# Making the first FFN weight sums earlier, in a pool of their own, and taking the FFN's other sums off GpSimd

## The chip, the cores and the metric

The kernel runs on one core of a Trainium2 chip. The metric is the device time of one execution in microseconds; the median of the runs shown counts. The engines are called by their names or by the abbreviations of the profile: TensorE (PE), VectorE (DVE), ScalarE (ACT), GpSimd (POOL) and SyncE (SP), which issues the weight loads.

## The reference

One trunk layer on x of 512 frames by 1024 features, in float32. The change lies in the feed-forward network (FFN) at its end, where D_FF is 2816:

```python
def reference(x, ...):
    ...
        h = h + (g_a * ya + g_b * yb) @ w_o[l]
        hn = rmsnorm(h, norm_ffn_g[l])
        gu = hn @ w_ffn_in[l]
        g, up = jnp.split(gu, 2, axis=-1)
        h = h + (jax.nn.silu(g) * up) @ w_ffn_out[l]
    return rmsnorm(h, final_norm_g)
```

Ahead of it stand a norm, one wide input projection, chunked band attention, an RG-LRU branch and the gated merge of the two.

## The kernel before, in words

**Products in three parts.** Every float32 operand is split into a high part (`hi`, rounded by a ScalarE copy) and a low part (`lo`, the rest, by a VectorE subtraction; `split`, lines 78 to 81). A product is three matmuls, hi·hi, hi·lo and lo·hi (`mm3`, lines 72 to 76). So each weight tile costs one load on SP's queue, one ScalarE copy and one VectorE subtraction before TensorE may use it, and the lo·hi matmul needs the subtraction as well.

**Weights.** `chunks` lists all weight blocks in order of use. `load` issues 512 KB into a `raw` buffer of the pool `wp` (three buffers; every fourth load of the FFN's Strassen blocks goes to a single buffer of the pool `sc`). `prefetch` keeps the split weights (`whl`, four buffers in `wp`) ahead of their use.

**The stage of w_o** (lines 746 to 763): four row tiles by two column halves; each psum result is added to `h` on VectorE (line 756), squared and summed on ScalarE. After two row tiles the FFN norm's first half follows (`norm_half`, TensorE transposes at line 326), and the second half later.

**The FFN's first two blocks** fg0 and fu0 are multiplied plainly, half of the rows before and half after the second norm half (`po_f0` to `po_f3`).

**The FFN's other blocks**, fg2, fu2, fg4 and so on to fu20, use a Strassen–Winograd scheme: seven products in place of eight. It needs four sums of the activations, t1 to t4 (lines 810 to 820: `sum_t`, split into `bt0` to `bt3`), and for each block four sums of its weight quarters (`weight_sums`, lines 158 to 188): s1 = a21 + a22, s2 = s1 − a11, s3 = a11 − a21, s4 = a12 − s2. The plain quarters a11, a12 and a22 and the four sums are each split. `block_product` (lines 240 to 263) then runs seven products of 12 matmuls (128x128 by 128x256). One psum tile, `p`, gathers a11·b11, + s2·t2, + s3·t3, + a22·t4, and after each of them ScalarE copies the state so far (`keepa`, `keepb`, c); the other, `q`, takes a12·b21, s1·t1 and s4·b22:

```python
        product(p[:], w["s2"], right["t2"], False)
        keep(a[:, 1], p[:])
        product(q[:, 1], w["s1"], right["t1"], True)
        keep(b[:, 0], q[:, 1])
        product(p[:], w["s3"], right["t3"], False)
        keep(b[:, 1], p[:])
```

**What sets the order.** A planner orders the instructions of each engine before the kernel runs, so the order in the profile can differ from the program's; each engine then works through its list in order. Buffers come free tile by tile: whoever needs one waits until the last reader of its former tile is done.

**What GpSimd does in the FFN before:** s3 and s4 of fg2, fu2 and fg4 (lines 172 and 173), the four operations of t3 and t4 (line 805, called from 813 and 814), and the low part of `bt3` (line 819).

Of the kernel before, what the change touches and what calls it, by code (L numbers as in the profile page):

```python
# [8 lines left out]
F32 = mybir.dt.float32  # L9
F32R = mybir.dt.float32r  # L10
# [4 lines left out]
P = 128  # L15
# [17 lines left out]
CW = 256  # L33
# [3 lines left out]
def block_kernel(ctx: ExitStack, tc: tile.TileContext, x, norm_mix_g, w_in, b_merge, rel_table,  # L37
# [3 lines left out]
    pe, dve, act, pool, sp = nc.tensor, nc.vector, nc.scalar, nc.gpsimd, nc.sync  # L41

    def pool_of(name, bufs=1, side="left"):
        return tc.tile_pool(name=name, bufs=bufs, side=side, reuse_waits="tile")

    def opened(name, bufs=1, side="left"):
        st = ExitStack()
        return st, st.enter_context(pool_of(name, bufs, side))
# [6 lines left out]
    wp = ctx.enter_context(pool_of("wp", 2))  # L55
# [10 lines left out]
    def f(ap):  # L66
        return ap.bitcast(F32)

    def mm_tile(name, tag="mm"):
        return ps.tile([P, S], F32, tag=tag, bufs=4 if tag == "mm" else 2, name=name)  # L70
# [7 lines left out]
    def split(hi, lo, src):  # L78

        act.activation(hi, src, AF.Copy)  # L80
        dve.tensor_sub(lo, src, f(hi))  # L81
# [52 lines left out]
    raws = {}  # L134
    extra = {}

    def load(name, k):
        _, parts, rows, kts = chunks[index[name]]
        wide = sum(width for *_, width in parts)
        n = min(4 * CW // wide, kts - k)  # L140
        at = rows + k * P
        pl, bufs = wp, 3
        if name in strassen and name[0] == "f":
            loads[0] += 1
            pl, bufs = (room[0], 1) if loads[0] % 4 == 0 else (wp, 3)
        raw = pl.tile([P, n, wide], F32, tag="raw", bufs=bufs, name=f"raw_{name}_{k}")
        to = 0
        for src, col, width in parts:
            sp.dma_start(out=raw[:, :, to:to + width],
                         in_=src[at:at + n * P, col:col + width].rearrange("(k p) e -> p k e", p=P))  # L150
            to += width
        raws[name, k] = raw

    slots, loads = [0], [0]
    barrier = ["wo1"]
    room = [None]

    def weight_sums(name):

        for k in (0, 4):  # L160
            if (name, k) not in raws:
                load(name, k)
        r0, r1 = raws.pop((name, 0)), raws.pop((name, 4))
        a11, a21, a12, a22 = r0[:, :, 0:P], r0[:, :, P:CW], r1[:, :, 0:P], r1[:, :, P:CW]
        sc = room[0]
        s21, s34 = (sc.tile([P, 2, 4, P], F32, tag=tag, bufs=1, name=f"{tag}_{name}")
                    for tag in ("s21", "s34"))
        s2, s1, s3, s4 = s21[:, 0], s21[:, 1], s34[:, 0], s34[:, 1]
        dve.tensor_add(s1, a21, a22)
        dve.tensor_sub(s2, s1, a11)  # L170
        other = pool if name in ("fg2", "fu2", "fg4") else dve
        other.tensor_sub(s3, a11, a21)
        other.tensor_sub(s4, a12, s2)
        blocks_ = {}
        for group in ((("a11", a11), ("a12", a12)), (("s2", s2), ("s1", s1)), (("s3", s3), ("s4", s4)), (("a22", a22),)):
            pl, tag, bufs = sc, "a22", 2
            if len(group) == 2:
                slots[0] += 1
                pl, tag, bufs = (sc, "whl", 1) if slots[0] % 5 == 0 else (wp, "whl", 4)
            o = pl.tile([P, len(group), 2, 4, P], F32R, tag=tag, bufs=bufs, name=f"whl_{name}_{group[0][0]}")  # L180
            together = group[0][0] in ("s2", "s3") and name != "fg2"
            if together:
                split(o[:, :, 0], o[:, :, 1], (s21 if group[0][0] == "s2" else s34)[:])
            for i, (key, src) in enumerate(group):
                if not together:
                    split(o[:, i, 0], o[:, i, 1], src)
                blocks_[key] = o[:, i]
        return blocks_

    def prefetch(n):  # L190
        while len(made) < min(n, len(chunks), index.get(barrier[0], len(chunks))):
            name, parts, rows, kts = chunks[len(made)]
            if name in strassen:
                made.append(weight_sums(name))
                continue
            tiles = []
            wide = sum(width for *_, width in parts)
            step = 4 * CW // wide
            for k in range(0, kts, step):
                n_ = min(step, kts - k)  # L200
                if name in extra:
                    hl = extra[name].tile([P, 2, n_, wide], F32R, tag="whl", bufs=4, name=f"whl_{name}_{k}")
                else:
                    hl = wp.tile([P, 2, n_, wide], F32R, tag="whl", bufs=4, name=f"whl_{name}_{k}")
                if (name, k) not in raws:
                    load(name, k)
                raw = raws.pop((name, k))
                if len(made) == 0 and k:
                    act.activation(hl[:, 0], raw[:], AF.Copy)
                    pool.tensor_sub(hl[:, 1], raw[:], f(hl[:, 0]))  # L210
                else:
                    split(hl[:, 0], hl[:, 1], raw[:])
                tiles.append(hl)
            made.append(lambda part, k, at, tiles=tiles, step=step: tiles[k // step][:, part, k % step, at])

    def weights(name, ahead=1):
        prefetch(index[name] + 1 + ahead)
        return made[index[name]]
# [116 lines left out]
    def features(pl, tag, name):  # L335

        t = pl.tile([P, KT, 2, S], F32R, tag=tag, name=name)
        return t, [t[:, k] for k in range(KT)]
# [13 lines left out]
    _, xnT = features(xnp, "xn", "xnT")  # L352
# [361 lines left out]
    _, mT = features(xnp, "xn", "mT")  # L714
# [16 lines left out]
        act.dma_start(out=ht[t][:], in_=x[t * P:(t + 1) * P, :])  # L731


    x32_stack, x32p = opened("x32", 1, "right")
    bl = {(kh, half): (x32p if (kh, half) == (0, 1) else hnp).tile([P, 2, 4, 256], F32R, name=f"hn{kh}{half}")
          for kh in range(2) for half in range(2)}
# [7 lines left out]

    hsq = []
    prefetch(index["wo1"] + 1)
    for t in range(NT):
        q2 = cp.tile([P, 2], F32, tag="hsq2", bufs=2, name=f"hsq2_{t}")
        for cc in range(2):
            wo = weights(f"wo{cc}", 0)  # L750
            po = mm_tile(f"po_h{cc}_{t}")
            for k in range(KT):
                mm3(po[:], mT[k][:, 0, t * P:(t + 1) * P], mT[k][:, 1, t * P:(t + 1) * P],
                    wo(0, k, every), wo(1, k, every), k == 0, k == KT - 1)
            hs = ht[t][:, cc * S:(cc + 1) * S]
            dve.scalar_tensor_tensor(hs, po[:], 0.5, hs, ALU.mult, ALU.add)
            junk = tg_.tile([P, S], F32, tag="tg", name=f"hj{t}_{cc}")
            act.activation(junk[:], hs, AF.Square, accum_out=q2[:, cc:cc + 1])
        q = cp.tile([P, 1], F32, tag="ssq", bufs=4, name=f"hsq{t}")
        dve.tensor_reduce(q[:], q2[:], mybir.AxisListType.X, ALU.add)  # L760
        hsq.append(q[:])
        if t == 1:
            norm_half(x32p, ht, hsq, gf, hn_at, 0, "ffn", f_at)
# [2 lines left out]


    acp = ctx.enter_context(pool_of("act", 13))
    bt_stack, btp = opened("bt")
    act2 = []  # L770

    def act_tile(j):
        o = acp.tile([P, 2, S], F32, tag="act", name=f"act{j}")
        act2.append(o)
        return o
# [20 lines left out]
    def sums(name):  # L796
        t = acp.tile([P, 4, 256], F32, tag="act", name=f"sum_{name}")
        return t

    def of_x(kh, half, i):  # L800
        return x32[2 * kh + i][:, :, half * 256:half * 256 + 256]

    def halves_of(dst, op, in0, in1):
        for i in range(2):
            op(dst[:, 2 * i:2 * i + 2], in0(i), in1(i))

    def own_half(t):
        return lambda i: t[:, 2 * i:2 * i + 2]

    t1, t2, t3, t4 = (sums(f"t{i}") for i in range(1, 5))  # L810
    halves_of(t1, dve.tensor_sub, lambda i: of_x(0, 1, i), lambda i: of_x(0, 0, i))
    halves_of(t2, dve.tensor_sub, lambda i: of_x(1, 1, i), own_half(t1))
    halves_of(t3, pool.tensor_sub, lambda i: of_x(1, 1, i), lambda i: of_x(0, 1, i))
    halves_of(t4, pool.tensor_sub, lambda i: of_x(1, 0, i), own_half(t2))
    bt = []
    for i, t in enumerate((t1, t2, t3, t4)):
        o = btp.tile([P, 2, 4, 256], F32R, name=f"bt{i}")
        act.activation(o[:, 0], t[:], AF.Copy)
        (pool if i == 3 else dve).tensor_sub(o[:, 1], t[:], f(o[:, 0]))
        bt.append(o)  # L820
    hn_right = right_side(lambda kh, half, part, k: bl[kh, half][:, part, k], bt)
    x32_stack.close()
    sc_stack, sc = opened("sc", 2)
# [23 lines left out]
    for j in range(2, FT, 2):  # L847
# [4 lines left out]
        o = act_tile(j)[:].rearrange("p a b -> p (a b)")  # L852
# [2 lines left out]
        dve.tensor_mul(o, o, u[:].rearrange("p a b -> p (a b)"))  # L855
    sc_stack.close()
    bt_stack.close()
    hn_stack.close()


# [97 lines left out]
```

## Time and profile before

| | |
|---|---|
| median of 3 runs | 892.38 us (891.75 to 892.43) |
| the profiled execution | 892.82 us |
| its span, first to last instruction | 891.0 us |
| mean granted TensorE clock | 0.996 |
| TensorE busy | 875.7 us (98%) |
| VectorE busy | 553.5 us (62%) |
| ScalarE busy | 473.2 us (53%) |
| GpSimd busy | 130.2 us (15%) |

The times and tables below come from one profiled execution. In a timeline a row has the start and the duration in us, the engine, the source line, the operation and its output and inputs by the program's names without numbers; in square brackets at the end stands how long the engine had idled before, and what ended that. Rows of several like instructions in sequence are merged (x2 and so on). Group rows have the count, then the busy time in us and the mean of one in ns. The stage of w_o runs from about 486 to 532 us, the FFN's plain blocks up to 556, the Strassen blocks from there to about 768, and the output projection from 760 on.

### The profile page before, as it was taken

The numbers are of one execution on the slowest core, as the hardware profiler recorded it, in microseconds if no ns is written. First come the engines' busy times: TensorE is split into PE (matmuls) and PEld (weight loads), VectorE is DVE, ScalarE is ACT, GpSimd is POOL, SyncE is SP. The second block draws the span as 40 slices with busy tenths as digits, with TensorE's granted clock in tenths as the row PEclk, the third lists the DMA queues.
The fourth block names the chain that finished last, engine by engine and source line by source line (L and its number), as shares of the span: only waits on it lengthen the run. The fifth ranks groups of instructions, "written<-read, shape, count | busy, mean of one in ns | idle before, by whom it ended". The sixth has DMA issues, their size and how long they took to land.

```text
span 891.0 us, 13319 instructions
## 1 busy us (share of the span) xinstructions
PE 875.7 (98%) x5220; PEld 779.4 (87%) x5220; DVE 553.5 (62%) x863; ACT 473.2 (53%) x841; POOL 130.2 (15%) x168
## 2 busy tenths in 40 slices
PE   8999999999999999999999999899999999999997
PEld 5988888888889889898888889899999999888886
DVE  5777557563466675666456356998788887463203
ACT  7566646652266676667434366556655556723203
POOL 4012112120022222323000003400000001300200
PEclk9999999999999999999999999899999999999999
DMA  8323223333332232331224430333333333253102
GB/s 264 89 79 111 82 91 95 120 95 95 106 104 74 77 101 72 94 96 61 71 85 145 172 95 25 95 119 116 122 95 95 97 115 101 97 187 125 37 1 96
DMA packets 85024, 89.06 MB, mean 100 GB/s; under 512 B 5344, under 2 KB 73552, under 8 KB 84960
## 3 DMA queue, kind: packets, MB, share of 16 engines
q1 hardware_dynamic: 83584, 84.73, 30.7%
q10 hardware_dynamic: 1376, 3.47, 1.0%
q8 instruction: 41, 0.67, 0.3%
q14 instruction: 23, 0.19, 0.1%
HBM read 86.05 MB, written 2.14 MB: 99 GB/s over the span
## 4 chain that ended last, share of the span: by engine, by line
PE 94%; DVE 3%; ACT 1%; issue 1%; DMA 1%; POOL 0%; SPq 0%; ACTq 0%
PE po_out L74 5%; PE po_out L76 5%; PE po_out L75 5%; PE p_fu L75 2%; PE p_fu L74 2%; PE o L663 2%; PE p_fu L76 2%; PE p_fg L75 2%; PE p_fg L76 2%; PE p_fg L74 2%; PE pT L643 2%; PE po_v L76 2%; PE po_v L75 2%; PE po_v L74 2%; PE po_q L74 2%; PE q_fg L76 2%
## 5 line engine op out<-in xcount | busy, mean ns | idle before, releaser
L75 PE MATMUL po_out<-whl_fo,act_hi 128*128 128x512 f32 (+1 forms) x198 | 72.4, 366 | 0.0
L74 PE MATMUL po_out<-whl_fo,act_hi 128*128 128x512 f32 (+1 forms) x198 | 72.4, 366 | 0.0
L76 PE MATMUL po_out<-whl_fo,act_lo 128*128 128x512 f32 (+1 forms) x198 | 71.6, 365 | 0.0
L631 POOL TENSOR_SCALAR p<-p,rl 128x128 f32<-128x128 f32 (+1 forms) x64 | 35.9, 583 | 142.0 <-DVE rl L629 142.0
L81 DVE TENSOR_TENSOR whl_fo<-raw_fo,whl_fo 128x1024 fp32r<-128x1024 f32 x22 | 27.6, 1261 | 45.5 <-ACT whl_fo L80 45.1
L80 ACT ACTIVATE whl_fo<-raw_fo 128x1024 fp32r<-128x1024 f32 x22 | 22.9, 1056 | 49.3 <-PE po_out L76 35.0
L627 DVE CUSTOM_DVE_ANT_0 p<-s,bias 128x384 f32<-128x384 f32 (+2 forms) x64 | 29.5, 484 | 21.5 <-PE s L625 20.9
L76 PEld LDWEIGHTS po_out<-whl_fo,act_lo 128*128 128x128 f32 x198 | 37.3, 189 | 6.0
L75 PEld LDWEIGHTS po_out<-whl_fo,act_hi 128*128 128x128 f32 x198 | 37.4, 189 | 6.0
L74 PEld LDWEIGHTS po_out<-whl_fo,act_hi 128*128 128x128 f32 x198 | 37.4, 189 | 6.0
L628 ACT ACTIVATE p<-p,m 128x384 f32<-128x384 f32 (+2 forms) x64 | 35.7, 560 | 12.6 <-DVE m L627 12.2
L843 POOL TENSOR_TENSOR act_lo<-act,act_hi 128x1024 fp32r<-128x1024 f32 x4 | 10.5, 2621 | 185.9 <-ACT act_hi L842 184.4
L76 PE MATMUL po_v<-whl_v,xnT 128*128 128x256 f32 x128 | 36.2, 283 | 0.0
L75 PE MATMUL po_v<-whl_v,xnT 128*128 128x256 f32 x128 | 36.1, 282 | 0.0
L74 PE MATMUL po_v<-whl_v,xnT 128*128 128x256 f32 x128 | 36.1, 282 | 0.0
L81 DVE TENSOR_TENSOR pp<-pT,pp 128x512 fp32r<-128x512 f32 (+1 forms) x64 | 29.3, 484 | 5.3 <-ACT pp L80 5.0
L81 DVE TENSOR_TENSOR whl_fu_s<-s_fu,whl_fu_s 128x1024 fp32r<-128x1024 f32 x20 | 25.3, 1280 | 5.8 <-ACT whl_fu_s L80 5.7
L75 PE MATMUL po_xr<-xnT,whl_xr 128*128 128x512 f32 (+1 forms) x80 | 27.9, 354 | 0.6 <-DVE xnT L331 0.6
L74 PE MATMUL po_gr<-xnT,whl_gr 128*128 128x512 f32 (+1 forms) x80 | 27.8, 349 | 0.1
L76 PE MATMUL po_gr<-xnT,whl_gr 128*128 128x512 f32 (+1 forms) x80 | 27.5, 348 | 0.3 <-DVE whl_gr L81 0.3
L75 PE MATMUL po_gr<-xnT,whl_gr 128*128 128x512 f32 (+1 forms) x80 | 27.6, 346 | 0.0
L74 PE MATMUL po_xr<-xnT,whl_xr 128*128 128x512 f32 (+1 forms) x80 | 26.6, 351 | 0.8 <-ACT xnT L330 0.8
(354 smaller groups left out, 3077.1 us busy)
## 6 DMA issues: line engine op xcount, KB each, us to landing
raw_fg<-in_w_ffn_in_dram SPq DMA_DIRECT2D x22, 512.0 KB, 4.4
raw_fu<-in_w_ffn_in_dram SPq DMA_DIRECT2D x22, 512.0 KB, 3.5
raw_fo<-in_w_ffn_out_dram SPq DMA_DIRECT2D x22, 512.0 KB, 4.0
raw_qk<-in_w_in_dram SPq DMA_DIRECT2D x32, 256.0 KB, 3.2
raw_xr<-in_w_in_dram SPq DMA_DIRECT2D x8, 512.0 KB, 4.6
raw_gr<-in_w_in_dram SPq DMA_DIRECT2D x8, 512.0 KB, 3.5
raw_ga<-in_w_in_dram SPq DMA_DIRECT2D x8, 512.0 KB, 3.9
raw_gb<-in_w_in_dram SPq DMA_DIRECT2D x8, 512.0 KB, 3.5
```

The costliest lines, as they stand in the source:

```text
L74: pe.matmul(o, sh, mh, start=start, stop=False, skip_group_check=parts)
L75: pe.matmul(o, sh, ml, start=False, stop=False, skip_group_check=parts)
L76: pe.matmul(o, sl, mh, start=False, stop=stop, skip_group_check=parts)
L80: act.activation(hi, src, AF.Copy)
L81: dve.tensor_sub(lo, src, f(hi))
L627: dve.tensor_tensor_reduce(prob[qb][:], sc[:, 0:w], bias[:, S - w:S], -1.0, 3e38, ALU.add, ALU.min, nmax[:, qb:qb + 1])
L628: act.activation(prob[qb][:], prob[qb][:], AF.Exp, bias=nmax[:, qb:qb + 1], scale=-1.0, accum_out=lsum[:, qb:qb + 1])
L631: pool.tensor_scalar(prob[qb][:], prob[qb][:], rl[:, qb:qb + 1], 1.0, ALU.mult, ALU.mult)
L643: pe.transpose(pt[:, at * P:(at + 1) * P], prob[qb][:, kb * P:(kb + 1) * P], ident[:])
L663: pe.matmul(po[:, S - n:S], st, pp[i][:, part, lo:lo + n], start=kb == 0 and part == 0, stop=kb == NT - 1 and part == 1)
L843: (pool if i in (0, 1, 2, 4) else dve).tensor_sub(lo[:], o[:], f(hi[:]))
```

## The change

A new pool `sums` is opened on the right side before the norm's tiles and closed after the Strassen blocks. It holds the two tiles of sums (`s21`, `s34`) of every block, and one buffer of split weights that the pool `sc` held before.

`weight_sums("fg2", True)` is called right behind the prefetch of w_o. It loads fg2 (two loads of 512 KB), makes its four sums, splits s2 and s1 in one piece and keeps s3 and s4. When fg2's turn comes in `prefetch`, its weights are loaded a second time, for a11, a12 and a22, which now go into spare tiles of the activation pool (`acp`); s3 and s4 are split from what was kept. All of s3 and s4, t3, t4 and the low part of `bt3` are made on VectorE; GpSimd has none of them. The pool of every fifth split pair is counted differently, in step with the one made ahead.

```diff
+        if name not in begun:
+            a11, a21, a12, a22 = blocks_of()
+            s21, s34 = (sums_room.tile([P, 2, 4, P], F32, tag=tag, bufs=1, name=f"{tag}_{name}")
+                        for tag in ("s21", "s34"))
+            s2, s1, s3, s4 = s21[:, 0], s21[:, 1], s34[:, 0], s34[:, 1]
+            dve.tensor_add(s1, a21, a22)
+            dve.tensor_sub(s2, s1, a11)
+            dve.tensor_sub(s3, a11, a21)
+            dve.tensor_sub(s4, a12, s2)
+        if ahead:
+            slots[0] += 1
+            o = sums_room.tile([P, 2, 2, 4, P], F32R, tag="whl", bufs=1, name=f"whl_{name}_s2")
+            split(o[:, :, 0], o[:, :, 1], s21[:])
+            begun[name] = (s34, {"s2": o[:, 0], "s1": o[:, 1]})
+            return
         sc = room[0]
...
-        other = pool if name in ("fg2", "fu2", "fg4") else dve
-        other.tensor_sub(s3, a11, a21)
-        other.tensor_sub(s4, a12, s2)
         blocks_ = {}
+        if name in begun:
+
+            a11, a21, a12, a22 = blocks_of()
+            s34, blocks_ = begun.pop(name)
+            s1 = s2 = None
+            s3, s4 = s34[:, 0], s34[:, 1]
         for group in ((("a11", a11), ("a12", a12)), (("s2", s2), ("s1", s1)), (("s3", s3), ("s4", s4)), (("a22", a22),)):
+            if group[0][0] in blocks_:
+                continue
+            if name == "fg2" and group[0][0][0] == "a":
+
+                for key, src in group:
+                    o = spare[0].tile([P, 2, 4, P], F32R, tag="act", bufs=13, name=f"whl_{name}_{key}")
+                    split(o[:, 0], o[:, 1], src)
+                    blocks_[key] = o
+                continue
             pl, tag, bufs = sc, "a22", 2
             if len(group) == 2:
                 slots[0] += 1
-                pl, tag, bufs = (sc, "whl", 1) if slots[0] % 5 == 0 else (wp, "whl", 4)
+                pl, tag, bufs = (sums_room, "whl", 1) if slots[0] % 5 == 1 else (wp, "whl", 4)
...
-            together = group[0][0] in ("s2", "s3") and name != "fg2"
+            together = group[0][0] in ("s2", "s3")
...
+    sums_stack, sums_room = opened("sums", 1, "right")
...
     prefetch(index["wo1"] + 1)
+    weight_sums("fg2", True)
...
-    halves_of(t3, pool.tensor_sub, lambda i: of_x(1, 1, i), lambda i: of_x(0, 1, i))
-    halves_of(t4, pool.tensor_sub, lambda i: of_x(1, 0, i), own_half(t2))
+    halves_of(t3, dve.tensor_sub, lambda i: of_x(1, 1, i), lambda i: of_x(0, 1, i))
+    halves_of(t4, dve.tensor_sub, lambda i: of_x(1, 0, i), own_half(t2))
...
-        (pool if i == 3 else dve).tensor_sub(o[:, 1], t[:], f(o[:, 0]))
+        dve.tensor_sub(o[:, 1], t[:], f(o[:, 0]))
```

More of the change, by code (lines that the diff above doesn't have):

```diff
@@ L156, in block_kernel @@
     room = [None]
[L158 to L164, printed above, removed]
-        sc = room[0]
[L166 to L170, printed above, removed]
-        other = pool if name in ("fg2", "fu2", "fg4") else dve
-        other.tensor_sub(s3, a11, a21)
-        other.tensor_sub(s4, a12, s2)
-        blocks_ = {}
-        for group in ((("a11", a11), ("a12", a12)), (("s2", s2), ("s1", s1)), (("s3", s3), ("s4", s4)), (("a22", a22),)):
+    begun = {}
@@ new lines, in block_kernel, with weight_sums, blocks_of @@
+    spare = [None]
+    def weight_sums(name, ahead=False):
+        def blocks_of():
+            for k in (0, 4):
+                if (name, k) not in raws:
+                    load(name, k)
+            r0, r1 = raws.pop((name, 0)), raws.pop((name, 4))
+            return r0[:, :, 0:P], r0[:, :, P:CW], r1[:, :, 0:P], r1[:, :, P:CW]
+        if name not in begun:
[13 more added lines that the diff above has]
+            return
+        sc = room[0]
+        blocks_ = {}
+        if name in begun:
[3 more added lines that the diff above has]
+            s3, s4 = s34[:, 0], s34[:, 1]
+        for group in ((("a11", a11), ("a12", a12)), (("s2", s2), ("s1", s1)), (("s3", s3), ("s4", s4)), (("a22", a22),)):
+            if group[0][0] in blocks_:
[6 more added lines that the diff above has]
+                continue
@@ L768, in block_kernel @@
     acp = ctx.enter_context(pool_of("act", 13))
+    spare[0] = acp
     bt_stack, btp = opened("bt")
@@ L857, in block_kernel @@
     bt_stack.close()
+    sums_stack.close()
     hn_stack.close()
```

## The prediction

> **What bounds the kernel now.** I read the span and clock of the core and the page first, then what TensorE waited for, then the one place where it waits long, on every engine.
>
> ```profile
> core 0: 891.0 us, clock 0.996
> ```
>
> ```profile
> PE 875.7 (98%) x5220; PEld 779.4 (87%) x5220; DVE 553.5 (62%) x863; ACT 473.2 (53%) x841; POOL 130.2 (15%) x168
> ...
> PE 94%; DVE 3%; ACT 1%; issue 1%; DMA 1%; POOL 0%; SPq 0%; ACTq 0%
> ```
>
> TensorE is busy for 98% and carries 94% of the chain that ended last. The change keeps all its matmuls, so all that can be won is TensorE's idle or slowed time. The view of what it waited for:
>
> ```profile
> PE s L624 <- ACT kh L586: 2.0, 4, 0.5
> PE q_fg L74 <- ACT whl_fg_s L80: 1.9, 1, 1.9
> PE q_fg L76 <- DVE whl_fg_s L81: 1.2, 1, 1.2
> ```
>
> The first line is four gaps of at most 0.5. The second and third are one long gap each, and they stand in one place: the first use of the sums of fg2, the first Strassen block. TensorE's timeline there (start, duration, instruction, idle before it):
>
> ```profile
> 554.86 0.28 PE L76 MATMUL po_f<-hn,whl_fu 128*128 128x256 f32 x1
> ...
> 559.18 0.28 PE L76 MATMUL q_fg<-hn,whl_fg_a 128*128 128x256 f32 x1
> 561.37 0.39 PE L74 MATMUL q_fg<-bt,whl_fg_s 128*128 128x256 f32 x1 [1.91 <-ACT whl_fg_s L80]
> 561.59 0.28 PE L75 MATMUL q_fg<-bt,whl_fg_s 128*128 128x256 f32 x1
> 563.11 0.58 PE L76 MATMUL q_fg<-bt,whl_fg_s 128*128 128x256 f32 x1 [1.24 <-DVE whl_fg_s L81]
> ...
> 567.76 0.41 PE L76 MATMUL p_fg<-bt,whl_fg_s 128*128 128x256 f32 x1
> ...
> 569.24 0.28 PE L76 MATMUL p_fu<-hn,whl_fu_a 128*128 128x256 f32 x1
> ```
>
> From 554.86 to 559.18 are 36 matmuls, a pitch of 0.12 us. From 561.37 up to 569.24 run 30 more; at that pitch, from 559.30 on, they would have been through at 562.90. So 569.24 − 562.90 = **6.34 us** are lost here: about 3.2 in the two waits, and about 3.1 afterwards, when each matmul takes 0.41. The stretches (length; busy time of PE, PEld, DVE, ACT, POOL; granted clock) say why:
>
> ```profile
> 547.00:580.00 33.00, 29.86 (x224) 29.45 (x224) 29.45 (x30) 18.75 (x33) 20.09 (x11) 0.90 0.27 84
> 567.00:569.00 2.00, 2.00 (x11) 2.00 (x11) 1.96 (x4) 0.39 (x2) 0.56 (x1) 0.50 0.43 146
> 600.00:740.00 140.00, 140.00 (x1169) 140.00 (x1169) 116.67 (x162) 81.65 (x150) 0.00 (x0) 1.00 0.34 106
> ```
>
> After the waits the granted clock is 0.50 until about 569. At 600 to 740, without GpSimd, nothing is lost. GpSimd's 11 operations of 547 to 580, 20.09 us, are exactly those that the change takes off it. Two of them, the VectorE operations beside them, ScalarE's, and one VectorE form there and later:
>
> ```profile
> 556.74 3.37 POOL L819 TENSOR_TENSOR bt<-sum_t,bt 128x1024 fp32r<-128x1024 f32 x1
> 562.53 1.67 POOL L173 TENSOR_TENSOR s_fg<-raw_fg,s_fg 128x512 f32<-128x512 f32 x1 [2.43 <-DVE s_fg L170]
> ```
>
> ```profile
> 557.78 2.87 DVE L169 TENSOR_TENSOR s_fg<-raw_fg,raw_fg 128x512 f32<-128x512 f32 x1
> ...
> 562.38 0.68 DVE L81 TENSOR_TENSOR whl_fg_s<-s_fg,whl_fg_s 128x512 fp32r<-128x512 f32 x1
> 562.98 1.77 DVE L81 TENSOR_TENSOR whl_fu_a<-raw_fu,whl_fu_a 128x512 fp32r<-128x512 f32 x1
> ...
> 589.05 1.22 DVE L81 TENSOR_TENSOR whl_fu_s<-s_fu,whl_fu_s 128x1024 fp32r<-128x1024 f32 x1
> ```
>
> ```profile
> 560.68 0.63 ACT L80 ACTIVATE whl_fg_s<-s_fg 128x512 fp32r<-128x512 f32 x1 [3.54 <-DVE s_fg L169]
> ...
> 568.21 0.38 ACT L248 ACTIVATE keepa_fg<-p_fg 128x256 f32<-128x256 f32 x1 [2.12 <-PE p_fg L76]
> ```
>
> ```profile
> L81 DVE TENSOR_TENSOR whl_fg_a<-raw_fg,whl_fg_a 128x512 fp32r<-128x512 f32 x6 | 7.4, 1273 | 0.8 <-ACT whl_fg_a L80 0.8
> ...
> L81 DVE TENSOR_TENSOR whl_fg_a<-raw_fg,whl_fg_a 128x512 fp32r<-128x512 f32 x21 | 14.2, 685 | 2.0 <-ACT whl_fg_a L80 1.9
> ```
>
> A VectorE operation takes 0.68 alone (six that meet GpSimd take 1.27 on average, 21 later ones 0.685). The sum at 557.78 takes 2.87 and ends at 560.65, 0.54 after GpSimd's 3.37 end at 560.11; the one at 562.98 ends at 564.75, 0.55 after GpSimd's at 564.20. The late sum holds ScalarE's copy at 560.68, and that copy holds TensorE. So the cause reads as: GpSimd holds up VectorE, VectorE makes the first sums late, and the gap costs the clock. The Trainium skill ("SBUF — State Buffer", section "SBUF: two separate sides") calls the port pair of VectorE and GpSimd "an exclusive lock, not a bandwidth split" for a VectorE operation with two inputs in SBUF; the trace agrees, by the 0.54 and 0.55.
>
> **The change, part by part.**
>
> *Removed: the 6.34 us.* In the changed kernel's instruction order, TensorE is the same up to the first fg2 matmul (24 matmuls end with 559.18's, so it starts at 556.42). Then come p_fg2 a11 (12), p_fu2 a11 and q_fu2 a12 (24), two of q_fu2 s1, two of q_fg2 a12, ten of q_fu2 s1, then p_fg2 s2 and s3, ten of q_fg2 a12, q_fg2 s1, p_fg2 a22, q_fg2 s4. Whether it waits is decided by VectorE's list, which I lay out by hand at a pitch of 0.60 for 128x512 (562.38 to 562.98) and 1.22 − 0.08 = 1.14 for 128x1024. GpSimd's 11 operations cost VectorE 10 × 0.60 + 1.14 = 7.1, where GpSimd's presence stretched it by about as much: of 29.45 busy us, the 30 operations at own pitch would need some 20. At 555.2 it is through with a11 and a12 of fu2. Up to fg2's a22 there follow five of 1.14 (bt1, bt2, fu2's s2, bt3, fu2's s3) and five of 0.60 (two of act0, a22 of fu2, a12 and a22 of fg2): 555.2 + 5.7 + 3.0 = 563.9. TensorE's needs: fu2's s2 lows (done 558.7) at 561; bt2 (557.5) at 563.9; a12 of fg2 (563.3) at 565.9; all held. So none of the 6.34 comes back as a late sum.
>
> *Added under w_o: four sums, one 1024 split, two loads.* VectorE has room:
>
> ```profile
> 501.44 0.69 DVE L756 SCALAR_TENSOR_TENSOR h<-po_h,h 128x512 f32<-128x512 f32 x1 [1.83 <-PE po_h L76]
> ...
> 529.93 21.37 SPq L149 DMA_DIRECT2D raw_fu<-in_w_ffn_in_dram  x2
> 537.42 1.04 PE L326 MATMUL pt_ffn<-ident,xs_ffn 128*128 128x128 f32 x8
> DMA to landing us min/median/max: 3.4/4.4/4.7
> ```
>
> (VectorE, SP's queue, TensorE, and the tile view of raw_fg.) The sums take 4 × 0.60 = 2.4 us, in the order right ahead of the addition at 501.44, before which VectorE idles 1.83; the addition comes about 0.6 later, and TensorE uses what follows from it only after the next tiles. The split's lows (1.14) go behind that addition, where VectorE idles again. On SP's queue fg2's loads take the places of fg0's, and fg0, fu0 and fu2 move two places back; all but one have over 10 us left. The exception: fu2's second half, issued at 529.93, lands at 533.3 to 534.6, and fu2's s1 on VectorE now waits for it ahead of the last norm: behind it stand that norm's sum, fu2's s2, a reciprocal and xs_ffn, some 2.2 us together. So xs_ffn is there at 535.5 to 536.8, and TensorE transposes it from 537.42 on: nothing, with 0.6 of cover. Bounds: zero and, for a landing as far over 4.7 as 4.7 is over 3.4, 0.7.
>
> *Added: fg2 is loaded again (1 MB) for a11, a12 and a22.* The second half waits in SP's queue for a raw buffer that the matmul at 554.86 frees: issued 555.2, landed 558.6 to 559.9, ScalarE's a12 copy (0.63) done at 559.3 to 560.6, and TensorE needs it after 38 matmuls, at 556.42 + 4.56 = 560.98. Behind that copy stands keepa of p_fg2, done by 561.5, needed at 562.4. Then fg4's second half has to wait for the single buffer of its pool, which fg2's a22 frees at 563.9; it lands at 567.3 to 568.6; ScalarE's fg4 a22 copy and, behind it, keepb of q_fg2 are done by 569.6; TensorE needs keepb's buffer at 570.0. Both fit, with 0.4 us of cover at the worst landing. Taken: 0; bounds 0 and, for one landing a microsecond or two later than any shown, 3.
>
> *A new wait.* p_fg2 s3 follows p_fg2 s2 at once, into the psum tile that keepa must first copy. Before, others stood in between (that at 569.24 is one). ScalarE starts 568.21 − 567.76 = 0.45 after the last matmul's start and takes 0.38, and some 0.06 until TensorE goes; less the pitch of 0.12 that would have gone by anyway: 0.45 + 0.38 + 0.06 − 0.12 = 0.77, at the full clock 0.13 less (0.28 for 0.41): **0.64**. Bounds: 0.5 and 1.0. Does this gap lower the clock? TensorE's four gaps of 0.5 (kh) are the nearest row, and they didn't: a mean clock of 0.996 leaves 0.004 × 891 = 3.6 us short of full, and the one interval at 0.50, some 6 to 7 us by TensorE's rows, takes 3.0 to 3.5 of that. Taken: no.
>
> *After 570.* VectorE needs 116.67 of 140 us where it has the same work per block, so any lag melts at 1.7 us per block of ten. The out stage keeps its order.
>
> **Sum**, against the profiled execution, 892.82 us (span 891.0 and 1.8 around it): 892.82 − 6.34 + 0.64 = 887.1. That execution lies 0.44 over the median of 892.38; against the median **886.7 us**.
>
> **Rivals.**
> 1. *The second loading is late.* fg2's second half, fg4's second half or the fg4 blocks behind them miss TensorE by 1 to 3 us. For: three covers of 0.4 to 0.9 in a list made by hand, each on one landing. Against: landings of 3.4 to 4.7 were used at their worst. Time 886.7 + 1 to 3: **888 to 890**.
> 2. *The same, and the clock halves again.* From a wait of about 2 us on, 3.1 is added: 886.7 + 2 to 3 + 3.1 = **about 892**, no change. For: in the trace the clock went at 1.91 + 1.24. The Trainium skill ("TensorE: Matmul & The Clock Gate", Part 1, "The HAM clock gate") lets the clock fall only after a whole idle window of about 3.4 us. The trace differs: no idle stretch here was that long, the longest was 1.91. By that rule a single wait of 2 us would keep the clock, and this rival would fall back to the first, at about 889.
> 3. *VectorE becomes the bound; slower.* If the stretched operations are not GpSimd's doing (memory traffic, say), VectorE keeps its pace and takes 7.1 us more. fg2's a22 is then done at 571 instead of 563.9, fg4's second half lands at 575.7, and keepb is missed by 6.7 at 570.0, with the clock halved: 886.7 + 6.7 + 3.1 = **896.5**. It decides from 565 on: a22 later than that makes keepb late. For: 30 operations fill 29.45 of 33 us. Against: 21 of the same form at 0.685 under a higher DMA share (0.34 against 0.27), and the two ends at 0.54 and 0.55.
> 4. *The wait at s3 is hidden* (or keepa is quicker): **886.0**. That the sums are not made early is excluded, since the changed kernel's order has them between the splits of w_o and the second h addition.
>
> **Chances.** Forecast 0.58, rival 4 0.06, rival 1 0.16, rival 2 0.08, rival 3 0.12. A measurement of this kernel can tell about 0.2%, 1.8 us, from no change: faster is below 890.6, slower above 894.2. Forecast, 4 and 1 are faster: 0.80; rival 2 the same: 0.08; rival 3 slower: 0.12. The range takes in the forecast with the bounds of the s3 wait, rival 4 and rival 1, so 885.5 to 890.5, and leaves 0.20 out. The likeliest case's own range is 886 to 887.5.
>
> **What would show it.** Right: TensorE has no wait of over 1 us from 547 on; one of about 0.6 before p_fg2's s3 put down to keepa; the granted clock is 1.00 throughout 547 to 580; GpSimd is idle there; VectorE's 128x512 operations take 0.68 throughout; the span is about 885.3. Wrong: a wait on a copy behind raw_fg2_4 or raw_fg4_4, or on keepb (1, 2); VectorE's operations still over 1 us without GpSimd (3); a new wait at pt_ffn around 537.

## The result and the profile after

The changed kernel takes **887.26 us** (median of 4, 887.22 to 887.70); the kernel before, with one more run, 892.15 us (median of 4, 891.75 to 892.43). The ratio is 0.9947, 95% interval 0.9929 to 0.9964: 4.9 us less, clear of the 0.2% named in the prediction. The forecast was 886.7, in a range of 885.5 to 890.5. The kernel before spreads over more than a microsecond: of 20 later runs ten took 891.58 to 891.81, at a mean granted clock of 0.996 or 0.997, and ten 892.32 to 892.81, at 0.995 or 0.996. The profiled execution of the changed kernel took 887.22 us.

Busy time by engine, and what TensorE waited for (in us: total, times, longest); dots mark lines left out:

```profile
span 885.4 us, 13311 instructions
...
PE 871.9 (98%) x5220; PEld 776.5 (88%) x5220; DVE 548.4 (62%) x872; ACT 472.7 (53%) x839; POOL 112.1 (13%) x157
```

```profile
PE s L651 <- ACT kh L613: 2.0, 4, 0.5
...
PE p_fg L74 <- ACT keepa_fg L275: 0.5, 1, 0.5
```

The span was to be 885.3 and is 885.4. The two long waits on the sums of fg2 are gone, and at the place one wait is left, the one foretold before p_fg2's s3. VectorE is busy for less time than before, 548.4 us against 553.5, with 9 operations more. TensorE's timeline at that wait, and the stretches (length; busy time of PE, PEld, DVE, ACT, POOL; granted clock; DMA share; GB/s):

```profile
563.59 0.28 PE L76 MATMUL p_fg<-bt,whl_fg_s 128*128 128x256 f32 x1
564.34 0.38 PE L74 MATMUL p_fg<-bt,whl_fg_s 128*128 128x256 f32 x1 [0.47 <-ACT keepa_fg L275]
```

```profile
547.00:580.00 33.00, 32.53 (x271) 32.32 (x270) 28.11 (x40) 19.76 (x35) 0.00 (x0) 1.00 0.40 126
600.00:740.00 140.00, 140.00 (x1169) 140.00 (x1169) 116.87 (x161) 81.36 (x148) 2.42 (x1) 1.00 0.33 103
```

From 547 to 580 the clock is 1.00, GpSimd does nothing, and TensorE idles just for these 0.47 us. VectorE now does 40 operations in 28.11 us where 30 filled 29.45. The VectorE form that the prediction shows twice (`whl_fg_a`), VectorE's list up to fg2's a22 and two operations behind it, and then ScalarE:

```profile
L81 DVE TENSOR_TENSOR whl_fg_a<-raw_fg,whl_fg_a 128x512 fp32r<-128x512 f32 x6 | 4.0, 686 | 0.0
```

```profile
555.20 2.35 DVE L851 TENSOR_TENSOR bt<-sum_t,bt 128x1024 fp32r<-128x1024 f32 x2
...
562.67 1.29 DVE L81 TENSOR_TENSOR whl_fg_a<-raw_fg,whl_fg_a 128x512 fp32r<-128x512 f32 x2
563.88 0.68 DVE L177 TENSOR_TENSOR s_fg<-raw_fg 128x512 f32<-128x512 f32 x1
567.78 0.69 DVE L175 TENSOR_TENSOR s_fg<-raw_fg,raw_fg 128x512 f32<-128x512 f32 x1 [3.23 <-DMA raw_fg<-in_w_ffn_in_dram]
```

```profile
558.88 1.15 ACT L80 ACTIVATE whl_fg_a<-raw_fg 128x512 fp32r<-128x512 f32 x2
560.53 0.39 ACT L275 ACTIVATE keepa_fg<-p_fg 128x256 f32<-128x256 f32 x1 [0.51 <-DVE act L865]
563.90 0.38 ACT L275 ACTIVATE keepa_fg<-p_fg 128x256 f32<-128x256 f32 x1 [2.98 <-PE p_fg L76]
```

Six of whl_fg_a take 686 ns where they took 1273. The list that was laid out by hand from 555.2 to 563.9 runs from 555.20 to 563.96.

### The profile page after: what moved, and what is told of

It is laid out like the page before. It is cut to its first block, busy times and chain, and to the rows that moved or that the text cites. A ratio compares the mean times of both kernels' runs of the same rounds, so it can differ in the third digit from the quotient of the medians.

```text
span 885.4 us, 13311 instructions
## 1 busy us (share of the span) xinstructions
PE 871.9 (98%) x5220; PEld 776.5 (88%) x5220; DVE 548.4 (62%) x872; ACT 472.7 (53%) x839; POOL 112.1 (13%) x157
## 4 chain that ended last, share of the span: by engine, by line
PE 96%; DVE 1%; SPq 1%; DMA 1%; ACT 1%; issue 1%; POOL 0%; ACTq 0%
PE po_out L74 5%; PE po_out L75 5%; PE po_out L76 5%; PE p_fg L74 2%; PE o L690 2%; PE p_fg L76 2%; PE p_fu L76 2%; PE p_fu L75 2%; PE p_fg L75 2%; PE p_fu L74 2%; PE pT L670 2%; PE po_v L75 2%; PE po_v L76 2%; PE po_v L74 2%; PE po_q L74 2%; PE po_q L75 2%
## 5 line engine op out<-in xcount | busy, mean ns | idle before, releaser
L81 DVE TENSOR_TENSOR whl_fg_s<-s_fg,whl_fg_s 128x1024 fp32r<-128x1024 f32 x20 | 25.6, 1295 | 3.7 <-ACT whl_fg_s L80 3.7
```

## The experiments

The theory: GpSimd's operations hold VectorE up, so the first sums came late, TensorE waited, and the gap lowered its clock. The rivals: that it is the early sums that count; that only GpSimd's own results were late, not VectorE's; that memory traffic did it. The change does two things at once, so each was run alone first.

### Off GpSimd only

```diff
-        other = pool if name in ("fg2", "fu2", "fg4") else dve
+        other = dve
...
-    halves_of(t3, pool.tensor_sub, lambda i: of_x(1, 1, i), lambda i: of_x(0, 1, i))
-    halves_of(t4, pool.tensor_sub, lambda i: of_x(1, 0, i), own_half(t2))
+    halves_of(t3, dve.tensor_sub, lambda i: of_x(1, 1, i), lambda i: of_x(0, 1, i))
+    halves_of(t4, dve.tensor_sub, lambda i: of_x(1, 0, i), own_half(t2))
...
-        (pool if i == 3 else dve).tensor_sub(o[:, 1], t[:], f(o[:, 0]))
+        dve.tensor_sub(o[:, 1], t[:], f(o[:, 0]))
```

> The kernel before, with only the 11 operations of the FFN taken off GpSimd and put on VectorE; no early sums, no pool of their own, no second loading. Theory (GpSimd held VectorE up, and that made fg2's first sums late): without GpSimd, VectorE's list of this kernel, laid out at 0.60 and 1.14 per operation, has fg2's s1 low part at about 560.2, where TensorE wants it at 559.5: one wait of about 0.7 us, no fall of the clock, so 892.4 - 6.3 + 0.7 = 886.5 to 887.5, that is as fast as the whole change. Rival (the early sums under w_o are what counts, since VectorE with 7.1 us more work would be later still): fg2's sums miss TensorE by more than before, 892 to 899.

Measured: 888.17 us against 892.07, ratio 0.9961 (0.9947 to 0.9975). So this part alone, without any early sum, brings 3.9 us where the whole change brings 4.9. VectorE is busy for 550.5 us with 11 operations more, against 553.5 in the kernel before. The time lies above the 886.5 to 887.5 expected, since the wait on the sums is longer than the 0.7 laid out:

```profile
559.34 0.68 DVE L81 TENSOR_TENSOR whl_fg_a<-raw_fg,whl_fg_a 128x512 fp32r<-128x512 f32 x1
559.94 0.68 DVE L833 TENSOR_TENSOR act<-tf,po_f 128x512 f32<-128x512 f32 x1
560.54 0.68 DVE L170 TENSOR_TENSOR s_fg<-s_fg,raw_fg 128x512 f32<-128x512 f32 x1
561.14 0.68 DVE L81 TENSOR_TENSOR whl_fg_s<-s_fg,whl_fg_s 128x512 fp32r<-128x512 f32 x1
```

```profile
561.88 0.39 PE L76 MATMUL q_fg<-bt,whl_fg_s 128*128 128x256 f32 x1 [1.64 <-DVE whl_fg_s L81]
```

VectorE runs at its own pace, but in this order s1's low part starts at 561.14, behind a22, act0 and s2, where I had it at about 560.2: a wait of 1.64. The clock did not fall after it (1.00 from 560 to 570). This is what the early sums are good for: they take the last wait on fg2's sums away, for some 0.9 us between the two medians, which come from two sessions.

### The early sums only

The changed kernel with `pool` back in all the places of the diff above.

> The changed kernel with the 11 operations back on GpSimd: only the early sums, their pool and the second loading. Theory: GpSimd still stretches VectorE's operations (0.68 to over 1 us between 547 and 562), but VectorE's list up to fu2's s2 low part is now 7.6 us long at its own pace and TensorE wants that part at 561.0, 13.6 us after its start; so the stretch is mostly covered, with waits of 0 to 2 us: 886.7 to 889. Rival (taking the work off GpSimd is what counts): the waits return in another place with the lowered clock, 890 to 893.

Measured: 893.25 us, ratio 1.0012 (1.0002 to 1.0021): nothing won, slightly slower. My expectation missed; the rival's holds in kind, at the upper end of its 890 to 893. TensorE's waits, and VectorE and GpSimd ahead of them:

```profile
PE q_fu L76 <- DVE whl_fu_s L81: 2.7, 1, 2.7
...
PE p_fg L74 <- ACT keepa_fg L275: 1.1, 1, 1.1
```

```profile
556.04 3.49 DVE L81 TENSOR_TENSOR whl_fu_a<-raw_fu,whl_fu_a 128x512 fp32r<-128x512 f32 x2
559.45 1.21 DVE L851 TENSOR_TENSOR bt<-sum_t,bt 128x1024 fp32r<-128x1024 f32 x1
560.59 4.51 DVE L81 TENSOR_TENSOR whl_fu_s<-s_fu,whl_fu_s 128x1024 fp32r<-128x1024 f32 x2
```

```profile
560.15 2.73 POOL L851 TENSOR_TENSOR bt<-sum_t,bt 128x1024 fp32r<-128x1024 f32 x1 [1.17 <-ACT bt L850]
```

The same delay in another place: two splits that take 1.29 together in the changed kernel take 3.49, and fu2's sums are now the ones that are late: TensorE waits 2.73 for them, and the clock is at 0.50 soon after. (The planner also orders TensorE otherwise here than in the changed kernel.) With the delay still there, the early sums only choose whom it hits.

### Unused work on GpSimd

Three kernels add to the changed one GpSimd work on a tile of its own, used by nobody. In the first two TensorE's, VectorE's, ScalarE's and SyncE's instructions stand in the same order, and only the kind of GpSimd's differs.

```diff
+    scr = acp.tile([P, 2, S], F32, tag="act", name="scr")
+    pool.tensor_sub(scr[:, 1].rearrange("p (a b) -> p a b", a=2), of_x(1, 1, 0), of_x(0, 1, 0))
+    pool.tensor_sub(scr[:, 0], scr[:, 1], scr[:, 1])
+    for i_ in range(11):
+        pool.tensor_sub(scr[:, 0], scr[:, 0], scr[:, 1])
```

> The changed kernel plus 13 GpSimd subtractions of 128x512 on a tile of their own, from about 547 us on, whose results nobody uses and nobody waits for; the planner's order of TensorE around fg2 is a little other than in the changed kernel, with matmuls between p_fg2's s2 and s3. Theory (GpSimd's operations themselves hold VectorE up): VectorE's 128x512 operations between 547 and 567 take 1 to 2.9 us instead of 0.68, fu2's s2 low part comes 3 to 7 us late, TensorE waits and the clock falls: 892 to 898. Rival (only the lateness of GpSimd's own results mattered, not its running): nothing changes, 886.5 to 887.5, VectorE's 128x512 at 0.68.

Measured: **903.75 us**, ratio 1.0134 (1.0119 to 1.0149), 16.5 us over the changed kernel and beyond the 898 that I had allowed. VectorE beside GpSimd, and TensorE's two longest waits:

```profile
562.32 1.75 DVE L81 TENSOR_TENSOR whl_fg_a<-raw_fg,whl_fg_a 128x512 fp32r<-128x512 f32 x1
563.99 1.75 DVE L837 TENSOR_TENSOR sum_t<-x,sum_t 128x512 f32<-128x512 f32 x1
565.66 2.30 DVE L856 TENSOR_TENSOR bt<-sum_t,bt 128x1024 fp32r<-128x1024 f32 x1
567.88 1.74 DVE L177 TENSOR_TENSOR s_fu<-raw_fu 128x512 f32<-128x512 f32 x1
```

```profile
L846 POOL TENSOR_TENSOR scr<-scr 128x512 f32<-128x512 f32 x11 | 19.2, 1749 | 0.9
```

```profile
PE p_fg L76 <- DVE whl_fg_a L81: 6.3, 1, 6.3
PE p_fu L76 <- DVE whl_fu_a L81: 5.3, 1, 5.3
```

Nobody waits for the results of these operations, so lateness of GpSimd's own results can't be it. Nor can DMA: from 555 to 565 the DMA share in this run is 0.00, and VectorE's operations take 1.75 there. A VectorE operation of 128x512 now lasts as long as one of GpSimd's does on average (1.75). Not all of the 16.5 us are the subtractions' doing, since the planner's order differs from the changed kernel's too; the third kernel below tells how much. The second kernel has memsets in place of the 11 subtractions of the loop:

```diff
-        pool.tensor_sub(scr[:, 0], scr[:, 0], scr[:, 1])
+        pool.memset(scr[:], float(i_))
```

> The same kernel as the one with the unused GpSimd subtractions, with the same order of instructions on TensorE, VectorE, ScalarE and SyncE, but 11 of the 13 are GpSimd memsets of 128x1024, which write and read nothing. Theory (VectorE is held up where GpSimd reads): only the first two, subtractions, cost VectorE something, up to 1.5 us and covered: 886.5 to 888, VectorE's 128x512 at 0.68 beside the memsets. Rival (any GpSimd operation holds VectorE up, writing ones too): VectorE is stretched as long as the memsets run, and the time is as in the run with subtractions, or between.

Measured: 892.08 us, ratio 1.0001 (0.9992 to 1.0011). VectorE's durations came as expected, the time did not. GpSimd, VectorE and TensorE:

```profile
550.86 11.07 POOL L846 MEMSET scr<- 128x1024 f32 x11
```

```profile
549.82 1.52 DVE L837 TENSOR_TENSOR sum_t<-x,sum_t 128x512 f32<-128x512 f32 x1
...
558.29 0.68 DVE L177 TENSOR_TENSOR s_fu<-raw_fu 128x512 f32<-128x512 f32 x1
558.89 0.68 DVE L178 TENSOR_TENSOR s_fu<-raw_fu,s_fu 128x512 f32<-128x512 f32 x1
559.49 1.28 DVE L81 TENSOR_TENSOR whl_fu_a<-raw_fu,whl_fu_a 128x512 fp32r<-128x512 f32 x2
```

```profile
560.23 0.39 PE L76 MATMUL p_fu<-hn,whl_fu_a 128*128 128x256 f32 x1 [1.82 <-DVE whl_fu_a L81]
...
567.07 0.58 PE L74 MATMUL p_fg<-bt,whl_fg_s 128*128 128x256 f32 x1 [2.51 <-ACT keepa_fg L275]
```

Beside the memsets VectorE runs at 0.68. But the two subtractions ahead of them had put it some 2 us back, and this order has fu2's a11 with no cover. I had called that covered without laying the order out. A third kernel tells the two apart: 13 memsets started by a ScalarE copy, and no subtraction.

> As the run with memsets, but without its first two GpSimd subtractions: the 13 memsets of 128x1024 are started by a ScalarE copy. The planner's order of TensorE and VectorE around fg2 is that of the two runs before with unused GpSimd work, which has act0 late on VectorE. Theory (writing alone holds VectorE up by nothing; the two subtractions held it up by 1.9 us): the wait of 1.8 us on fu2's a11 goes, the wait of about 2.5 us on keepa, which stands behind act0 in that order, and the fall of the clock stay: 892.1 - 1.8 = 890.0 to 890.8; VectorE's 128x512 at 0.68 from 547 on. Rival (the memsets did it): 892 and both waits as they were.

Measured: 890.81 us, ratio 0.9984 (0.9974 to 0.9994), at the upper end of the theory's range. The wait on fu2's a11 is gone, that on keepa (2.51) stands:

```profile
565.25 0.40 PE L74 MATMUL p_fg<-bt,whl_fg_s 128*128 128x256 f32 x1 [2.51 <-ACT keepa_fg L275]
```

```profile
548.30 13.13 POOL L845 MEMSET scr<- 128x1024 f32 x13 [112.58 <-ACT scr L843]
```

```profile
L837 DVE TENSOR_TENSOR sum_t<-x,sum_t 128x512 f32<-128x512 f32 x4 | 2.7, 684 | 0.0
```

While 13 us of memsets run, VectorE keeps 684 ns, its time with GpSimd idle. So GpSimd operations that read two operands hold these VectorE operations up, and ones that only write do not. The 3.5 us that this kernel still lies over the changed one are, by its rows, the order's: act0 stands late on VectorE, keepa behind it, and the clock falls after the wait of 2.51 us. TensorE's order is the same in all three of these kernels, so the 13 subtractions are best set against the 13 memsets: 903.75 − 890.81 = 12.9 us.

### Another buffer for the second loading

```diff
-            loads[0] += 1
-            pl, bufs = (room[0], 1) if loads[0] % 4 == 0 else (wp, 3)
+            loads[0] += room[0] is not None
+            pl, bufs = (room[0], 1) if loads[0] and loads[0] % 4 == 0 else (wp, 3)
```

> The changed kernel, with the two early loads of fg2 not counted in the turn by which every fourth load goes to the single buffer of the pool sc: fg2's second half goes to a buffer of wp and no longer has to wait for the last fu0 matmul at 555, and it is fu2's second half that waits there, as in the kernel before. The planner then puts fg2's a12 and s1 products ahead, with other matmuls between p_fg2's s2 and s3. Theory (the one wait left at fg2, 0.47 us before p_fg2's s3, comes from s3 following s2 at once): it goes, and VectorE's list has everything 0.5 us or more ahead of TensorE; 0.4 to 0.6 us less than the changed kernel, 886.5 to 887.0. Rival (another wait takes its place, on fu2's second half, landed at 558.6 to 559.9): 887.3 to 889.

> The changed kernel as it is, on the same chip as the run with the other raw buffer, to compare the two: 887.0 to 887.7.

Measured: 886.58 us (886.44 to 887.45, 5 runs) against the changed kernel's 887.43 (887.17 to 888.72, 5 runs) on the same chip; against the kernel before, 892.42 there, 0.9938 (0.9925 to 0.9950) and 0.9947 (0.9934 to 0.9961). Four of its five runs lie below the shortest of the changed kernel, though the intervals overlap, so a gain is likely and not more than that. What TensorE waited for, here and then in the changed kernel's new run:

```profile
PE s L651 <- ACT kh L613: 2.0, 4, 0.5
PE busy L301 <- DVE eps_t L307: 1.2, 1, 1.2
```

```profile
PE p_fg L74 <- ACT keepa_fg L275: 0.5, 1, 0.5
```

The wait before p_fg2's s3 is gone and nothing took its place. The span fell by about 1 us (885.7 to 884.6). Some 0.7 of it lies between the first Strassen matmul and the out stage, where this wait stood; the rest lies ahead of that, where the wait at pt_mix scatters between executions (1.1 in the changed kernel's and 0.3 in this one). Of all kernels run, this one has the lowest median.

## Why the prediction was right

**What bounds it, and the cause.** Right on each step, and now shown: the unused subtractions bring the stretched VectorE operations back, the memsets don't. The rule of the Trainium skill ("SBUF — State Buffer", section "SBUF: two separate sides", and its terms), that a two-input VectorE operation is shut out by a GpSimd operation that reads SBUF, and for that whole operation, agrees with both: 1.75 us beside reads of 1.75 on average, 0.68 beside memsets. Both sizes lose the same time, 0.68 to 1.75 and 1.22 to 2.30, that is 1.07 and 1.08 us: a wait of fixed length, not a slower pace, and near the 1.29 of GpSimd's shortest operation of that size with two operands in the kernel before. GpSimd, at 1.75 on average here, seems to wait in turn.

**The 6.34 us removed.** Right. VectorE's list ended at 563.96 as against 563.9 by hand. From the first p_fg2 matmul to the first of the out stage it is 203.61 us before (556.42 to 760.03) and 198.00 after (556.26 to 754.26): 5.61 less, where the sum had 5.70. The first of the out stage, before and after:

```profile
760.03 0.40 PE L74 MATMUL po_out<-whl_fo,act_hi 128*128 128x512 f32 x1
```

```profile
754.26 0.40 PE L74 MATMUL po_out<-whl_fo,act_hi 128*128 128x512 f32 x1
```

**The work under w_o.** Right at nothing: fu2's s1 did hold up the last norm, and xs_ffn was done at 536.86, just behind the forecast of 535.5 to 536.8; TensorE transposed from 537.25 without a wait, so 0.39 of cover was left of the 0.6.

**The second loading.** Right at nothing, with more cover than thought: ScalarE's copies of fg2's second half ran from 558.88, and fg4's second half, issued when a22 was done, had landed by 567.78, in the 567.3 to 568.6 foretold. So rivals 1 and 2 did not come about.

**The wait at s3.** Foretold at 0.64, as the time by which s3 starts later than at TensorE's pitch. By the rows it is 564.34 − (563.59 + 0.12) = 0.63; the profile's 0.47 counts from the end of a matmul of 0.28. ScalarE's copy takes its 0.38, and TensorE follows 0.06 after it, as in the sum.

**The size.** The medians moved by 4.9, the profiled executions by 5.6 (892.82 to 887.22), which is what the steps give. The rest is that the profiled execution of before, 892.82, lies above all four timed runs of before. The prediction took off its 0.44 over the median but counted the whole of its loss at fg2. Whether the loss at fg2 is smaller in other executions was not measured.

**Rival 3** fell with the list above; **that early sums alone would do** was never a step of the prediction, and the run shows that they don't.

## What to carry to other kernels

An engine that is busy for 15% of a kernel, but for 20.09 of the 33 us at the place that counts, can be the one that bounds, if its operations hold another one up: ask what stretches an operation that elsewhere takes 0.68 us before asking how to start it earlier. Work moved from GpSimd to VectorE can make VectorE finish sooner; here 11 operations more cost it nothing, and that part alone brought 3.9 us where the whole change brought 4.9. Laying the order out by hand, instruction by instruction, gave the size within 0.1 us between profiled executions; where I skipped that for an experiment (the early sums alone, the first memsets), I missed.

## What the runs showed of the clock

The clock falls after less idle time than I had reason to think. In the run with early sums alone (length; busy time of PE, PEld, DVE, ACT, POOL; granted clock; DMA share; GB/s):

```profile
564.50:565.00 0.50, 0.50 (x7) 0.50 (x6) 0.50 (x1) 0.00 (x0) 0.00 (x0) 1.00 0.00 0
565.00:565.50 0.50, 0.50 (x6) 0.50 (x5) 0.50 (x2) 0.00 (x0) 0.32 (x1) 0.98 0.00 0
565.50:566.00 0.50, 0.29 (x2) 0.00 (x1) 0.50 (x2) 0.00 (x0) 0.50 (x1) 0.50 0.00 0
...
572.00:572.50 0.50, 0.50 (x5) 0.50 (x5) 0.39 (x1) 0.45 (x1) 0.00 (x0) 0.69 0.00 0
```

The wait of 2.73 us ended at 564.01. The clock fell at about 565.48, when TensorE had been at work again for 1.5 us, and came back at about 572.31, 6.83 later. So here the fall did not come with the gap but behind it, as if idle time were judged over a stretch. Over the kernels, by the same view in half microseconds:

| kernel | waits at the place, us | idle in the 3.4 us before the fall | clock low for |
|---|---|---|---|
| before | 1.91, 1.24 | about 2.4 | about 6.8 |
| early sums only | 2.73, then 1.05 | about 1.9 | about 6.8 |
| memsets after two subtractions | 1.82, then 2.51 | about 2.2, in the second | about 3.4 |
| memsets alone | 2.51 | about 2.5 | about 3.4 |
| unused subtractions | 6.3, then 5.3 | 3.4 | about 13.7 |
| off GpSimd only, at fg2 | 1.64 | no fall | – |
| off GpSimd only, at the kernel's start | 0.87, 0.41 and part of 0.39 | about 1.5 | about 3.4 |

The last row is a fall at about 10.95 in that run's first microseconds; the stretch from 10 to 20 there:

```profile
10.00:20.00 10.00, 9.21 (x60) 8.66 (x61) 6.28 (x10) 9.22 (x18) 6.24 (x5) 0.83 0.86 260
```

In the third row the wait of 1.82 by itself lowered nothing, and in the changed kernel's profile about 1.9 us of idle time in 3.4 us (waits of 0.75, 0.71 and 0.41 between 6.3 and 9.5) lowered nothing either. So 1.5 us sufficed in one place and 1.9 did not in another: the amount alone does not decide. The Trainium skill ("TensorE: Matmul & The Clock Gate", Part 1, "The HAM clock gate") gives windows of about 3.4 us, one idle one for the fall and a busy one for the return. The lengths of the low clock agree: one, two or, with the unused subtractions, four such windows. A whole idle window was not needed here, where 1.5 to 2.5 us of idle time went ahead of the five other falls. Nor did a single wait cost the 3.1 us of lowered clock that rival 2 added for it: after the 2.51 us with memsets alone the clock was low for half as long as in the kernel before, by estimate about half of that price. Whether a wait of 2 us always costs this was not tried, since when in such a stretch a wait falls was not chosen.
